# V in two products of eight heads, the gates' logits in a product of their own, and the first norm's transposes amid the output projection

## The chip, the cores and the metric

The kernel runs on one core of a Trainium2 chip. The metric is device time: microseconds (us) of one execution of the whole program. The time before is the median of three runs, 662.65 us (662.37 to 663.92). The engines are PE (TensorE, the matrix engine; PEld is its loading of weights), ACT (ScalarE), DVE (VectorE), POOL (GpSimd) and SP (SyncE, which here only issues DMAs).

## The reference

One layer of a trunk: forgetting attention, a normalisation, a gated MLP with a causal depthwise convolution, a second normalisation and a gated embedding. There are 512 tokens, a width of 1024, 16 heads of 64, an MLP of 2816, all in float32. Cut to what matters here:

```
proj = x @ w_in                                    # 1024 -> 3*1024 + 16
q, k, v, f_logit = jnp.split(proj, [D_MODEL, 2 * D_MODEL, 3 * D_MODEL], axis=-1)
log_f = jax.nn.log_sigmoid(f_logit + b_f)          # one gate a token and head
c = jnp.cumsum(log_f, axis=1)
s = q k^T / 8 + c[query] - c[key]                  # causal
o = softmax(s) v
x = layer_norm(ALPHA * x + o @ w_out)
x = layer_norm(ALPHA * x + conv_ffn(x))            # gelu(conv(x w_up_g)) * (x w_up_u), then w_down
return x + sigmoid(x @ w_gate + b_gate) * (p @ w_proj)
```

## The kernel before

**Split products.** Every float32 operand of PE is cut in two parts of a narrower type, a high one (a copy on ACT) and a low one (the rest, a subtraction on DVE). `three` (L110) then makes a product out of three matmuls: high by high, high by low, low by high. Its flag `weights_move` says which operand stands in PE and which streams through it: with the flag, 128 tokens of x (or of the heads' outputs) stand and up to 512 columns of weights stream.

**Weights.** The class `Weights` (L52) keeps a list of slabs in the order in which they are used. `load_to` issues their DMAs into four buffers `raw`; `cut_to` cuts the next slab into `whi` (ACT, L93) and `wlo` (DVE, L94), five buffers each; `get` cuts one slab ahead and loads three further ones ahead. All DMAs are issued by SP, one after the other in program order. The tile framework's scheduler sets each engine's order from the order of the code, and frees buffers and banks as their readers finish.

**Attention.** `value_rows(n)` (L280) computes V of a group of heads for all four tiles of 128 tokens, in four PSUM banks `pv`. There are three groups (`V_HEADS`, L40): 4, 6 and 6 heads. The first carries the 16 columns of the gates' logits along, so that its rows are 272 wide; the other two are 384 wide. The first group runs at the very start, while x itself is still arriving and being cut (`load_x`, `cut_x`); its slabs hold one, one, two, two and two of the eight blocks of 128 rows (`k`). Its logits stand with tokens on partitions; four transposes (L436) turn them into `pf`, heads on partitions, from which L437 to L450 make the cumulated gates `cr`. `project(m, s)` computes queries or keys of two heads (`pp`, 24 matmuls of 512 columns). Then a loop over heads does scores (`s`), softmax, transposes (`t`) and values (`o`), each step a head behind the one before. Half of the output projection (columns 0 to 511, banks `ao`, `out_first`) runs between the last heads.

**Output projection and first norm.** The loop at L535 does the other half, bank `ap`, one token tile t at a time: 24 matmuls, then on DVE the addition to `y` (L496), statistics (L503, L507, L508), with a power on POOL (L509), and the normalisation (L510, L511, each 128x1024). `flip(t)` (L513) turns a normalised tile around for the MLP: twice four transposes on PE into a bank `nt` (L518), a high copy on ACT (`x1h`, L522) and a low part on DVE (`x1l`, L523). In the loop `flip` of tiles 0 and 1 is called behind all that belongs to tiles 2 and 3 (L546). Then the PSUM pool of eight banks (`first`) is closed, and a second of six banks `b` and two banks `gu` is opened (L550, L551). `flip` of tile 2 follows (L637), and that of tile 3 stands between products of the MLP.

**MLP.** It goes in four parts of up to six column blocks f. `up(f, s)` computes the gate side `g` (s = 0) or the other side `u` (s = 1) of a block, 24 matmuls; block 0, and `g` of block 1, go in two halves of 256 tokens, the first two halves ahead of `flip` of tile 3. The banks of f < 6 have the tag `b`, the later ones `gu`. `conv(f)` makes `a` out of `g`; `product(f)` multiplies it with `u` into `E` (L577). From part 1 on, the down products of the part before are woven in.

Of the kernel before, what the change touches and what calls it, by code (L numbers as in the profile page):

```python
# [8 lines left out]
F32 = mybir.dt.float32  # L9
F32R = mybir.dt.float32r  # L10
BF16 = mybir.dt.bfloat16
AF = mybir.ActivationFunctionType
# [3 lines left out]
P = 128  # L16
S = 512
D = 1024
H = 16
DH = 64  # L20
F = 2816
PLE = 256
NT = S // P
KD = D // P
# [12 lines left out]
UNIT = 1024  # L37
WARM = 14

V_HEADS = ((0, 4), (4, 6), (10, 6))  # L40

OUT_FIRST = {14: (0, 1), 15: (2, 3), 16: (4,), 17: (5, 6)}
RAW_BUFS = 4
# [59 lines left out]


@with_exitstack
def trunk_layer(ctx: ExitStack, tc: tile.TileContext, xT, x2d, pT, wqk, wv0, wv1, wv2, bf, wo, wup, cwb,
                wdn, wpl, wg, bg, gm, bm, gf, bff, out):
    nc = tc.nc

# [9 lines left out]
    first = ExitStack()  # L119
    psum = [first.enter_context(tc.tile_pool(name="psum", bufs=8, space=bass.MemoryType.PSUM))]  # L120

    def bank(name, tag="b", bufs=None):
        return psum[-1].tile([P, 512], F32, tag=tag, name=name, bufs=bufs)
# [2 lines left out]
        return w[k0 * P:(k0 + n) * P, cols * 512:(cols + 1) * 512].rearrange("(k p) c -> p k c", p=P)  # L126

    W = Weights(nc, base)
    wv = (wv0, wv1, wv2)
    u_v, u_qk = {}, []  # L130

    def add_v(n, pieces):
        k0, w = 0, wv[n].shape[1]
        for c in pieces:
            src = wv[n][k0 * P:(k0 + c) * P, :].rearrange("(k p) c -> p k c", p=P)
            u = W.add(src, n=c * w, inner=w)
            for j in range(c):
                u_v[n, k0 + j] = u, slice(j * w, j * w + w)
            k0 += c

    add_v(0, (1, 1, 2, 2, 2))
    for m in range(KD):
        u_qk.append([W.add(wqk[m, s], inner=P) for s in range(2)])
        if m == 0:
            add_v(1, (2, 2, 2, 2))
            add_v(2, (2, 2, 2, 2))

    u_o = [[W.add(half_rows(wo, 2 * j, 2, n), inner=512) for j in range(4)] for n in range(2)]

# [119 lines left out]
    load_x(2)  # L269
    load_x(3)  # L270
    W.load_to(3)
    nc.sync.dma_start(bf_sb, bf)
    cut_x(0, slice(0, P))
    W.cut_to(1)
    cut_x(0, slice(P, S))

    logits = {}
    fl_all = ap.tile([P, 128], F32, name="f", bufs=1)

    def value_rows(n):  # L280
        h0, nh = V_HEADS[n]
        w = wv[n].shape[1]
        pv = [bank(f"pv{t}_{n}") for t in range(NT)]
        for k in range(KD):
            if n == 0:
                if k + 4 < KD:
                    load_x(k + 4)
                if k + 1 < KD:
                    cut_x(k + 1)
            u, c = u_v[n, k]  # L290
            hi, lo = W.get(u)
            for t in range(NT):
                tk = slice(t * P, (t + 1) * P)
                three(pv[t][:, :w], hi[:, c], lo[:, c], xh[:, k, tk], xl[:, k, tk], k == 0,
                      k == KD - 1, weights_move=True)
        for t in range(NT):
            if n == 0:
                logits[t] = fl_all[:, t * H:t * H + H]
                nc.scalar.activation(logits[t], pv[t][:, nh * DH:w], AF.Copy)
            v = V[:, t, h0:h0 + nh]  # L300
            p3 = pv[t][:, :nh * DH].rearrange("p (h d) -> p h d", d=DH)
            nc.scalar.activation(v[:, :, 0, :], p3, AF.Copy)
            nc.vector.tensor_sub(v[:, :, 1, :], p3, v[:, :, 0, :].bitcast(F32))

    value_rows(0)

    KB = [ap.tile([P, S], F32R, name=f"KB{i}", bufs=1) for i in range(2)]
    QB = [ap.tile([P, S], F32R, name=f"QB{i}", bufs=1) for i in range(2)]
# [122 lines left out]
    cr = ap.tile([H, 4, S], F32R, name="cr", bufs=1)  # L431
    fa = ap.tile([H, S], F32, tag="KA", name="fa")
    fb = ap.tile([H, S], F32, tag="QA", name="fb")
    pf = bank("pf")
    for t in range(NT):
        nc.tensor.transpose(pf[:H, t * P:(t + 1) * P], logits[t], ident)  # L436
    nc.scalar.activation(fa, pf[:H], AF.Identity, bias=bf_sb)  # L437
    nc.vector.tensor_scalar_min(fb, fa, 0.0)
    nc.vector.scalar_tensor_tensor(fa, fb, -2.0, fa, op0=ALU.mult, op1=ALU.add)
    nc.scalar.activation(fa, fa, AF.Exp, scale=-1.0)  # L440
# [12 lines left out]
    stack(0)  # L453
    value_rows(1)
    stack(1)
    value_rows(2)
    for h in range(H + 2):
        m, s = divmod(h, 2)
        if h == 2:
# [33 lines left out]
    def add_half(t, n, ps, first):  # L493
        c = slice(n * 512, (n + 1) * 512)
        if first:
            nc.vector.scalar_tensor_tensor(y[:, t, c], y[:, t, c], ALPHA, ps, op0=ALU.mult, op1=ALU.add)  # L496
        else:
            nc.vector.tensor_add(y[:, t, c], y[:, t, c], ps)
# [3 lines left out]
            stats[t] = post.tile([P, 2, 6], F32, tag="st", name=f"st{t}", bufs=NT)  # L502
        nc.vector.bn_stats(stats[t][:, n, :], y[:, t, n * 512:(n + 1) * 512])  # L503

    def norm(t, g, b):
        mv = post.tile([P, 4], F32, tag="mv", name="mv", bufs=2)
        nc.vector.bn_aggr(mv[:, 0:2], stats.pop(t))  # L507
        nc.vector.tensor_scalar_add(mv[:, 2:3], mv[:, 1:2], EPS)  # L508
        nc.gpsimd.tensor_tensor(mv[:, 3:4], mv[:, 2:3], neghalf, op=ALU.pow)  # L509
        nc.vector.scalar_tensor_tensor(y[:, t], y[:, t], mv[:, 0:1], g, op0=ALU.subtract, op1=ALU.mult)  # L510
        nc.vector.scalar_tensor_tensor(y[:, t], y[:, t], mv[:, 3:4], b, op0=ALU.mult, op1=ALU.add)  # L511

# [22 lines left out]
    for t in range(NT):  # L535
        ps = bank(f"ap{t}")
        tk = slice(t * P, (t + 1) * P)
        for k in range(KD):
            hi, lo = W.get(u_o[1][k // 2])
            c = slice(k % 2 * 512, k % 2 * 512 + 512)  # L540
            three(ps, hi[:, c], lo[:, c], oh[:, k, tk], ol[:, k, tk], k == 0, k == KD - 1,
                  weights_move=True)
        add_half(t, 1, ps, True)
        half_stats(t, 1)
        norm(t, g1, b1)
        if t > 1:  # L546
            flip(t - 2, x1h, x1l)
    rows.close()
    oT.close()
    first.close()  # L550
    psum.append(ctx.enter_context(tc.tile_pool(name="psum2", bufs=6, space=bass.MemoryType.PSUM)))  # L551


    hpool = ctx.enter_context(tc.tile_pool(name="hpool", bufs=1, side="right"))
# [79 lines left out]
                        give(b, half, c)  # L634
                yield

    flip(2, x1h, x1l)  # L637
    before = None
    for part in range(4):
        if part < 3:  # L640
            shape = [P, len(PAIRS[0]), 7 * HALF]
        else:
            shape = [P, len(REST), S]
        hh, hl = [hpool.tile(shape, F32R, tag=g, name=f"{g}{part}", bufs=2) for g in ("hh", "hl")]
        slots = iter(CHUNKS[part] or ())

        def between():
            for _ in range(next(slots, 0)):
                next(before)

        for f in range(6 * part, min(6 * part + 6, NF)):
            q, j = f % 2, f // 2
            if q == 0:
                E = hpool.tile([P, 8 * HALF], F32, tag="E", name=f"E{j}")
            if f == 0:
                a, b = slice(0, HALF), slice(HALF, S)
                up(0, 0, a)
                up(0, 1, a)
                flip(3, x1h, x1l)
                up(1, 0, a)  # L660
                up(0, 0, b)
                up(0, 1, b)
                up(1, 0, b)
                conv(0)
                product(0, E[:, :S])
                continue
            if f > 1:
                up(f, 0)
            conv(f)
            between()  # L670
            up(f, 1)
            product(f, E[:, q * S:(q + 1) * S])
            if q:
                if part < 3:
                    operands(hh, hl, j - 3 * part, E)
                else:
                    i = f - 1 - REST[0]
                    e = E[:, :2 * S].rearrange("p (a b) -> p a b", b=S)
                    nc.scalar.activation(hh[:, i:i + 2], e, AF.Copy)
                    nc.vector.tensor_sub(hl[:, i:i + 2], e, hh[:, i:i + 2].bitcast(F32))  # L680
            between()
        if part < 3:
            before = down(part, hh, hl)
# [79 lines left out]
def _layout(a):  # L763
    import numpy as np

    c = np.ascontiguousarray
    w_in = a["attn_w_in"][0]
    qk = w_in[:, :2 * D].reshape(KD, P, 2, KD, P).transpose(3, 2, 1, 0, 4)
    wv = [w_in[:, 2 * D + h * DH:2 * D + (h + n) * DH] for h, n in V_HEADS]
    up = a["ffn_w_up"][0].reshape(KD, P, 2, NF, P).transpose(3, 2, 1, 0, 4)  # L770
    cw = np.concatenate([a["ffn_conv_w"][0], a["ffn_conv_b"][0][None]], 0)
    return {
        "xT": c(a["x"][0].T),
        "x2d": c(a["x"][0]),
        "pT": c(a["p"][0, 0].T),
        "wqk": c(qk),
        "wv0": c(np.concatenate([wv[0], w_in[:, 3 * D:]], 1)),
        "wv1": c(wv[1]),
        "wv2": c(wv[2]),
        "bf": c(a["attn_b_f"][0][:, None]),  # L780
        "wo": c(a["attn_w_out"][0]),
        "wup": c(up),
        "cwb": c(cw.reshape(4, NF, P).transpose(2, 1, 0)),
        "wdn": c(a["ffn_w_down"][0]),
        "wpl": c(a["ple_w_proj"][0]),
        "wg": c(a["ple_w_gate"][0]),
        "bg": c(a["ple_b_gate"][0][None]),
        "gm": c(a["ln_mix_g"][0][None]),
        "bm": c(a["ln_mix_b"][0][None]),
        "gf": c(a["ln_ffn_g"][0][None]),  # L790
        "bff": c(a["ln_ffn_b"][0][None]),
    }
# [16 lines left out]
```

## Time and profile before

The profiled execution took 664.75 us, 2.1 more than the median of the timed ones. Its trace spans 663.0 us.

| what | value |
|---|---|
| median of the timed runs | 662.65 us |
| profiled execution | 664.75 us |
| its span | 663.0 us |
| mean granted clock of PE | 0.997 |
| POOL's largest group, L377, softmax scaling | 72.9 us |
| DVE's largest group, L94, low parts of weights | 143.2 us |
| moved by DMA | 76.95 MB, mean 116 GB/s |

The busy time of an engine says how much of the span it worked; PE's matmuls overlap a little, so the length of a group of them is read from the chain of waits or from a timeline, not from the mean of one. In a timeline a row has its start, its length, the engine, the line, the operation and the operands, and in brackets how long the engine stood still ahead of it and for whom. The granted clock is the share of full speed at which PE ran.

### The profile page before, as it was taken

The page shows a single profiled execution, that of the slowest core. Times are in us where ns is not written, and L with a number is a line of the kernel's source. Part 1 is how long each engine was busy: PE and PEld are TensorE (multiplying, and loading weights), DVE is VectorE, ACT ScalarE, POOL GpSimd, SP SyncE. Part 2 cuts the span into 40 slices and gives each one's busy share as a digit, 9 for nine tenths or more (in the row PEclk, how much of TensorE's full clock was granted, in tenths as well). Part 3 has the DMA queues.
Part 4 walks back from the last instruction along what each step waited for, and adds up shares of the span by engine and source line. Part 5 has one row for each costly group of instructions (what it writes and reads, how often), then busy time and mean ns, then how long its engine had stood idle before and what let it go on. Part 6 is the DMA issues. An engine that isn't in the chain of part 4 may idle for free.

```text
span 663.0 us, 8693 instructions
## 1 busy us (share of the span) xinstructions
PE 654.0 (99%) x3234; PEld 558.0 (84%) x3234; DVE 474.0 (71%) x746; ACT 309.9 (47%) x511; POOL 85.2 (13%) x78
## 2 busy tenths in 40 slices
PE   8999999999999989999999999999999999999997
PEld 7899888888888879888888888888888888888886
DVE  7674789999986694755776675877667857599364
ACT  5653677787774232534434334443425343426231
POOL 0000554445444020000000000000000000012000
PEclk9999999999999998999999999999999999999999
DMA  8533221112262312322244244443363444562321
GB/s 272 176 129 128 64 66 64 40 61 66 66 228 74 128 54 77 128 96 95 86 137 160 95 153 134 158 128 111 96 189 111 129 142 128 158 223 65 102 81 47
DMA packets 32890, 76.95 MB, mean 116 GB/s; under 512 B 2960, under 2 KB 6800, under 8 KB 32848
## 3 DMA queue, kind: packets, MB, share of 16 engines
q1 hardware_dynamic: 32848, 76.41, 35.4%
q8 instruction: 25, 0.41, 0.3%
q14 instruction: 17, 0.14, 0.1%
HBM read 74.17 MB, written 2.10 MB: 115 GB/s over the span
## 4 chain that ended last, share of the span: by engine, by line
PE 95%; DVE 1%; ACT 1%; DMA 1%; issue 1%; SPq 0%; DVEq 0%
PE g L115 18%; PE u L115 18%; PE pp L115 13%; PE x L115 7%; PE gt L115 7%; PE pv L115 6%; PE z L115 4%; PE ao L115 3%; PE r L115 3%; PE o L403 3%; PE t L390 2%; PE ap L115 2%; PE y L115 2%; PE pl L115 2%; PE s L359 2%; PE s L361 1%
## 5 line engine op out<-in xcount | busy, mean ns | idle before, releaser
L93 ACT ACTIVATE whi<-raw 128x1024 fp32r<-128x1024 f32 (+5 forms) x131 | 126.3, 964 | 183.9 <-PE g L115 64.5
L94 DVE TENSOR_TENSOR wlo<-raw,whi 128x1024 fp32r<-128x1024 f32 (+5 forms) x131 | 143.2, 1099 | 67.7 <-ACT whi L93 67.1
L377 POOL TENSOR_SCALAR pr<-pr,rl 128x128 f32<-128x128 f32 (+1 forms) x64 | 72.9, 1157 | 134.7 <-DVE rl L373 134.7
L115 PE MATMUL g<-x1h,whi 128*128 128x512 f32 (+1 forms) x192 | 71.9, 375 | 0.0
L115 PE MATMUL g<-x1l,whi 128*128 128x512 f32 (+1 forms) x192 | 71.6, 373 | 0.0
L115 PE MATMUL g<-x1h,wlo 128*128 128x512 f32 (+1 forms) x192 | 71.6, 373 | 0.0
L115 PE MATMUL u<-x1h,whi 128*128 128x512 f32 (+1 forms) x184 | 69.9, 380 | 0.0
L115 PE MATMUL u<-x1l,whi 128*128 128x512 f32 (+1 forms) x184 | 69.9, 380 | 0.0
L115 PE MATMUL u<-x1h,wlo 128*128 128x512 f32 (+1 forms) x184 | 69.9, 380 | 0.0
L509 POOL TENSOR_TENSOR mv<-mv,neghalf 128x1 f32<-128x1 f32 x8 | 11.6, 1447 | 387.0 <-DVE mv L508 364.7
L115 PE MATMUL pp<-xh,wlo 128*128 128x512 f32 x128 | 50.2, 392 | 0.0
L115 PE MATMUL pp<-xl,whi 128*128 128x512 f32 x128 | 50.0, 391 | 0.0
L115 PE MATMUL pp<-xh,whi 128*128 128x512 f32 x128 | 49.9, 390 | 0.0
L115 PEld LDWEIGHTS g<-x1l,whi 128*128 128x128 f32 x192 | 36.6, 190 | 6.3
L115 PEld LDWEIGHTS g<-x1h,whi 128*128 128x128 f32 x192 | 36.6, 190 | 6.2
L115 PEld LDWEIGHTS g<-x1h,wlo 128*128 128x128 f32 x192 | 36.5, 190 | 6.2
L369 ACT ACTIVATE pr<-s,nm 128x128 f32<-128x128 f32 (+1 forms) x64 | 33.5, 526 | 16.9 <-DVE nm L368 15.8
L115 PEld LDWEIGHTS u<-x1l,whi 128*128 128x128 f32 x184 | 34.6, 188 | 6.6
L115 PEld LDWEIGHTS u<-x1h,whi 128*128 128x128 f32 x184 | 34.6, 188 | 6.5
L115 PEld LDWEIGHTS u<-x1h,wlo 128*128 128x128 f32 x184 | 34.6, 188 | 6.5
L577 DVE TENSOR_TENSOR E<-a,u 128x512 f32<-128x512 f32 x22 | 15.1, 687 | 34.2 <-PE u L115 33.4
L115 PE MATMUL pv<-whi,xh 128*128 128x384 f32 (+1 forms) x96 | 30.4, 330 | 1.1 <-ACT whi L93 1.1
(173 smaller groups left out, 1419.9 us busy)
## 6 DMA issues: line engine op xcount, KB each, us to landing
raw<-wup SPq DMA_DIRECT2D x44, 512.0 KB
raw<-wdn SPq DMA_DIRECT2D x31, 512.0 KB
raw<-wqk SPq DMA_DIRECT2D x16, 512.0 KB
raw<-wo SPq DMA_DIRECT2D x8, 512.0 KB
raw<-wg SPq DMA_DIRECT2D x8, 512.0 KB
raw<-wv SPq DMA_DIRECT2D x8, 384.0 KB
side<-wdn SPq DMA_DIRECT2D x9, 256.0 KB
raw<-wdn SPq DMA_DIRECT2D x9, 256.0 KB
```

The source lines that it names most:

```text
L93: self.nc.scalar.activation(hi[:, c:e], piece, AF.Copy)
L94: self.nc.vector.tensor_sub(lo[:, c:e], piece, hi[:, c:e].bitcast(F32))
L115: nc.tensor.matmul(ps, lhsT, rhs, start=start and n == 0, stop=stop and n == 2, skip_group_check=on)
L359: nc.tensor.matmul(ps[:, :n], QA[:, q], KA[:, :n], start=True, stop=False)
L361: nc.tensor.matmul(ps[:, :n], qb[0:68, q], kb[0:68, :n], start=False, stop=True)
L369: nc.scalar.activation(pr[:, off:off + w], ps[:, :w], AF.Exp, bias=nm[:, i:i + 1], accum_out=ls[:, i:i + 1])
L377: nc.gpsimd.tensor_scalar_mul(pr[:, off:off + w], pr[:, off:off + w], rl[:, i:i + 1])
L390: nc.tensor.transpose(ps[:, w:w + P], pr[:, o:o + P], ident)
L403: nc.tensor.matmul(ps[:, q0:], V[:, j, h], p[:, o:o + w], start=j == 0 and n == 0, stop=j == NT - 1 and n == 1)
L509: nc.gpsimd.tensor_tensor(mv[:, 3:4], mv[:, 2:3], neghalf, op=ALU.pow)
L577: nc.vector.tensor_mul(e, gates.pop(f), ups.pop((f, 1)))
```

## The change

V comes in two groups of eight heads, whose rows are 512 columns wide, a whole PSUM bank. The first has slabs of one, one, two, two and two blocks as before, the second four slabs of two. The logits get a product of their own behind the first group of V: a small tensor `fw` of 64 columns holds the high parts of their 16 weight columns in columns 0 to 15, the low parts in columns 32 to 47, and zeros elsewhere. `fw` stands in PE while x streams through it, 512 tokens at a time, low and high, for eight blocks: 16 matmuls. The result has heads on partitions, high part in rows 0 to 15 and low part in rows 32 to 47, which are added on DVE; the transposes and the copies of the logits are gone. In the output projection `flip` of tiles 0 and 1 moves ahead into the product of tiles 2 and 3, behind k = 3, and `flip` of tile 2 into `norm` of tile 3, ahead of its two normalising operations. The exchange of the PSUM pools moves from there to the start of part 1 of the MLP.

```
-V_HEADS = ((0, 4), (4, 6), (10, 6))
+V_HEADS = ((0, 8), (8, 8))
...
 @with_exitstack
-def trunk_layer(ctx: ExitStack, tc: tile.TileContext, xT, x2d, pT, wqk, wv0, wv1, wv2, bf, wo, wup, cwb,
+def trunk_layer(ctx: ExitStack, tc: tile.TileContext, xT, x2d, pT, wqk, wv0, wv1, wf, bf, wo, wup, cwb,
                 wdn, wpl, wg, bg, gm, bm, gf, bff, out):
...
     W = Weights(nc, base)
-    wv = (wv0, wv1, wv2)
+    wv = (wv0, wv1)
     u_v, u_qk = {}, []
...
             add_v(1, (2, 2, 2, 2))
-            add_v(2, (2, 2, 2, 2))
...
     W.load_to(3)
-    nc.sync.dma_start(bf_sb, bf)
     cut_x(0, slice(0, P))
...
-    logits = {}
-    fl_all = ap.tile([P, 128], F32, name="f", bufs=1)
+    wf_raw = ap.tile([P, KD * H], F32, name="wf", bufs=1)
...
         for t in range(NT):
-            if n == 0:
-                logits[t] = fl_all[:, t * H:t * H + H]
-                nc.scalar.activation(logits[t], pv[t][:, nh * DH:w], AF.Copy)
             v = V[:, t, h0:h0 + nh]
...
     value_rows(0)
+
+
+    nc.sync.dma_start(wf_raw, wf)
+    nc.sync.dma_start(bf_sb, bf)
+    fw = ap.tile([P, KD, 64], F32R, tag="QA", name="fw")
+    nc.vector.memset(fw.bitcast(F32), 0.0)
+    wf3 = wf_raw.rearrange("p (k h) -> p k h", h=H)
+    nc.scalar.activation(fw[:, :, 0:H], wf3, AF.Copy)
+    nc.vector.tensor_sub(fw[:, :, 32:32 + H], wf3, fw[:, :, 0:H].bitcast(F32))
+    pf = bank("pf")
+    for k in range(KD):
+        for n, x in enumerate((xl, xh)):
+            nc.tensor.matmul(pf[:64], fw[:, k, :], x[:, k, :], start=k == 0 and n == 0,
+                             stop=k == KD - 1 and n == 1)
...
     fb = ap.tile([H, S], F32, tag="QA", name="fb")
-    pf = bank("pf")
-    for t in range(NT):
-        nc.tensor.transpose(pf[:H, t * P:(t + 1) * P], logits[t], ident)
     nc.scalar.activation(fa, pf[:H], AF.Identity, bias=bf_sb)
+    nc.vector.tensor_add(fa, pf[32:32 + H], fa)
     nc.vector.tensor_scalar_min(fb, fa, 0.0)
...
     stack(1)
-    value_rows(2)
     for h in range(H + 2):
...
-    def norm(t, g, b):
+    def norm(t, g, b, meanwhile=None):
         mv = post.tile([P, 4], F32, tag="mv", name="mv", bufs=2)
...
         nc.gpsimd.tensor_tensor(mv[:, 3:4], mv[:, 2:3], neghalf, op=ALU.pow)
+        if meanwhile is not None:
+            flip(*meanwhile)
         nc.vector.scalar_tensor_tensor(y[:, t], y[:, t], mv[:, 0:1], g, op0=ALU.subtract, op1=ALU.mult)
...
                   weights_move=True)
+            if t > 1 and k == 3:
+                flip(t - 2, x1h, x1l)
         add_half(t, 1, ps, True)
         half_stats(t, 1)
-        norm(t, g1, b1)
-        if t > 1:
-            flip(t - 2, x1h, x1l)
+        norm(t, g1, b1, (2, x1h, x1l) if t == 3 else None)
     rows.close()
     oT.close()
-    first.close()
-    psum.append(ctx.enter_context(tc.tile_pool(name="psum2", bufs=6, space=bass.MemoryType.PSUM)))
...
-    flip(2, x1h, x1l)
     before = None
     for part in range(4):
+        if part == 1:
+            first.close()
+            psum.append(ctx.enter_context(tc.tile_pool(name="psum2", bufs=6, space=bass.MemoryType.PSUM)))
         if part < 3:
...
         "wqk": c(qk),
-        "wv0": c(np.concatenate([wv[0], w_in[:, 3 * D:]], 1)),
+        "wv0": c(wv[0]),
         "wv1": c(wv[1]),
-        "wv2": c(wv[2]),
+        "wf": c(w_in[:, 3 * D:].reshape(KD, P, H).transpose(1, 0, 2).reshape(P, KD * H)),
         "bf": c(a["attn_b_f"][0][:, None]),
```

On PE, at the end of the first group of V, this stood before (`pp_0` and `pp_1` are queries and keys of the first two heads; the three rows of a product repeat for each k):

```order
L115 MATMUL pp_0_317<-xh,wlo_254 128x512
L115 MATMUL pp_0_317<-xl,whi_253 128x512
L115 MATMUL pp_0_317<-xh,whi_253 128x512
L436 MATMUL pf<-ident,f 16x128 x4
L115 MATMUL pp_1_370<-xh,wlo_312 128x512
```

And now, there and at the end of `pv`:

```order
L115 MATMUL pv_0_131<-whi_218,xh 128x512
L115 MATMUL pv_0_131<-whi_218,xl 128x512
L115 MATMUL pv_0_131<-wlo_219,xh 128x512
L312 MATMUL pf<-xl,fw 64x512
L312 MATMUL pf<-xh,fw 64x512
...
L115 MATMUL pp_0_335<-xh,wlo_253 128x512
```

The four small transposes between queries and keys are gone; 16 matmuls of 512 columns stand ahead of both. The first group of V has 96 matmuls as before, now of 512 columns instead of 272; behind the keys there are 96 of 512 columns instead of 192 of 384.

On PE, from the output projection's last two tiles to the MLP's first product, this stood before (`ap_2532` is tile 2, `ap_2579` tile 3):

```order
L115 MATMUL ap_2532<-wlo_2468,oh 128x512
L518 MATMUL nt<-ident,y 128x128 x8
L115 MATMUL ap_2579<-whi_2371,oh 128x512
...
L115 MATMUL ap_2579<-wlo_2468,oh 128x512
L518 MATMUL nt<-ident,y 128x128 x16
L115 MATMUL g_2652<-x1h,whi_2479 128x256
```

And now (`ap_2414` is tile 2, `ap_2461` tile 3):

```order
L115 MATMUL ap_2414<-wlo_2326,oh 128x512
L525 MATMUL nt<-ident,y 128x128 x8
L115 MATMUL ap_2414<-whi_2337,oh 128x512
...
L115 MATMUL ap_2461<-wlo_2326,oh 128x512
L525 MATMUL nt<-ident,y 128x128 x8
L115 MATMUL ap_2461<-whi_2337,oh 128x512
...
L115 MATMUL ap_2461<-wlo_2350,oh 128x512
L525 MATMUL nt<-ident,y 128x128 x8
L115 MATMUL g_2530<-x1h,whi_2361 128x256
```

Two of the three groups of transposes now stand inside the products of tiles 2 and 3, 12 matmuls before their ends, and one group, not two, stands between the last product and the MLP.

On DVE the same stretch ends so before, from the last addition to the statistics of tile 3:

```order
L511 SCALAR_TENSOR_TENSOR y<-y,mv,b_2416 128x1024
L94 TENSOR_TENSOR wlo_2658<-raw_2471,whi_2657 128x1024
L496 SCALAR_TENSOR_TENSOR y<-y,ap_2579 128x512
L523 TENSOR_TENSOR x1l<-nt,x1h 128x4x128
L503 BN_STATS st_2440<-y 128x6
```

And now:

```order
L518 SCALAR_TENSOR_TENSOR y<-y,mv,b_2298 128x1024
L530 TENSOR_TENSOR x1l<-nt,x1h 128x4x128 x2
L501 SCALAR_TENSOR_TENSOR y<-y,ap_2461 128x512
L94 TENSOR_TENSOR wlo_2536<-raw_2353,whi_2535 128x1024
L508 BN_STATS st_2322<-y 128x6
L530 TENSOR_TENSOR x1l<-nt,x1h 128x4x128
```

Both low parts of tile 1 stand ahead of tile 3's addition, where before they stood behind it; the cut of a slab of weights stands between that addition and its statistics, and the low parts of tile 2 follow.

On PE, at the start of part 1 of the MLP, with what a row waits for in brackets (`u_3134` and `u_3012` are `u` of f = 5, `g_3175` and `g_3057` are `g` of f = 6), this stood before:

```order
L115 MATMUL u_3134<-x1l,whi_3067 128x512
L115 MATMUL u_3134<-x1h,wlo_3068 128x512
L115 MATMUL g_3175<-x1h,whi_3099 128x512 [waits Activation_49]
L115 MATMUL g_3175<-x1l,whi_3099 128x512
L115 MATMUL g_3175<-x1h,wlo_3100 128x512 [waits DVE_49]
```

And now:

```order
L115 MATMUL u_3012<-x1l,whi_2945 128x512
L115 MATMUL u_3012<-x1h,wlo_2946 128x512
L115 MATMUL g_3057<-x1h,whi_2977 128x512 [waits DVE_49]
L115 MATMUL g_3057<-x1l,whi_2977 128x512
L115 MATMUL g_3057<-x1h,wlo_2978 128x512
```

The products stand in the same order. Before, the first waited for the high part of its slab (ACT) and the third for the low part (DVE); now the first waits for DVE, at a count that is reached with the product `E` of f = 5 (L577 before, L582 now).

## The prediction

> **What bounds the kernel now.** I read each engine's share first, then the waits of PE, then the chain of waits in order of time, then the timelines of the three places that the change touches.
>
> ```profile
> PE 654.0 (99%) x3234; PEld 558.0 (84%) x3234; DVE 474.0 (71%) x746; ACT 309.9 (47%) x511; POOL 85.2 (13%) x78
> PE nt L518 <- DVE x1l L523: 2.7, 1, 2.7
> PE pv L115 <- ACT whi L93: 1.1, 2, 0.9
> PE warm L223 <- DVE zeros L219: 1.1, 1, 1.1
> ```
>
> PE is busy for 654.0 of 663.0 us (first line). The waits of PE (us in all, times, longest) name two besides the one ahead of the warm-up: 1.1 us for the first weights, 2.7 us at one group of transposes. So a change is worth what it takes out of PE's own stream and out of PE's waits; the other engines count where PE comes to wait for them.
>
> **What a product costs PE.** Durations of single matmuls overlap, so I take groups from the chain of waits: start, length, what, count.
>
> ```profile
> 17.81 1.51 PE pv L115 x12
> 25.16 0.44 PE pf L436 x4
> 25.60 5.46 PE pp L115 x24
> 31.06 33.30 PE pv L115 x192
> 225.02 14.07 PE ap L115 x62
> ```
>
> A 272-column product costs 1.51/12 = 0.126 us, one of 384 columns 33.30/192 = 0.173, one of 512 columns 0.227 (5.46/24, and 14.07/62 with x standing and the weights moving, the form of the new pv). Before: 96 x 0.126 + 192 x 0.173 = 45.4 us, and 0.4 for the four transposes of the logits. After: 192 x 0.227 = 43.6 us for V and 16 x 0.227 = 3.6 for the logits. No row shows 64 columns of weights standing; the bounds are 0.126 and 0.30 each, 2.0 to 4.8 us in all, and I take the 512-column price, since the moving side has that length. Sum: 47.2 - 45.8 = **1.4 us more PE work**: the logits' own product costs more than the 96 fewer products of V save.
>
> The Trainium skill, page "TensorE: Matmul & The Clock Gate", section "Wait — 56ns, not 53.3ns?", gives N/2.4 GHz plus about 2.5 ns from one warm matmul to the next. By that 272, 384 and 512 columns are 116, 163 and 216 ns, and the same sum comes to 2.2 us more. The rows above lie 11 to 13 ns over N/2.4 GHz, so here dropping a product is worth more than by the page, and the measured price stays.
>
> **The start.** Here PE waits for data, and the slabs of weights grow.
>
> ```profile
> 3.94 0.59 PE L115 MATMUL pv<-whi,xh 128*128 128x272 f32 x1
> 6.15 0.43 PE L115 MATMUL pv<-wlo,xh 128*128 128x272 f32 x1
> 6.38 0.42 PE L115 MATMUL pv<-whi,xl 128*128 128x272 f32 x1
> 10.29 0.39 PE L115 MATMUL pv<-whi,xh 128*128 128x272 f32 x1 [0.94 <-ACT whi L93]
> 4.07 5.49 DMA raw<-wv
> 9.58 0.66 ACT L93 ACTIVATE whi<-raw 128x544 fp32r<-128x544 f32 x1
> 13.65 1.06 ACT L93 ACTIVATE whi<-raw 128x1024 fp32r<-128x1024 f32 x1 [0.72 <-PE pv L115]
> 7.36:10.29 2.93, 1.99 (x12) 1.59 (x12) 1.82 (x4) 1.97 (x4) 0.00 (x0) 1.00 1.05 348
> 64.20 0.40 PE L359 MATMUL s<-KA,QA 128*128 128x256 f32 x2
> ```
>
> The third slab (k = 2 and 3) lands at 9.56 and is cut until 10.24; PE starts on it at 10.29 after 0.94 us of waiting and then runs without a gap to the first scores at 64.20. After the change the first three slabs carry 4 x 128 x 240 x 4 bytes = 0.49 MB more. At the 348 GB/s of that stretch (last column) this is 1.4 us, and the cut takes 1.06 for 0.66. So PE starts on it at 10.29 + 1.4 + 0.4 = 12.1, and I add 0.1 for its low half. Behind it stand 72 + 16 + 48 + 96 = 232 products of 512 columns, 52.6 us: first scores at 64.8, **+0.6 us**. Some of the 1.4 is paid out of the old wait.
> Lower bound: the slab is never late. The first product starts at about 4.5 (0.6 for the larger first slab and its cut); until 6.6 products run at half pace (6.15 to 6.38 is 0.23 us for 272 columns, against 0.126 later), that is five of them, and the other 19 of the first two slabs take 4.3: third slab at 11.0, so -0.6. Upper bound: the start loses as much as before (64.20 - 45.8 - 48 x 0.227 = 7.5 us), so the whole 1.4, and 0.6 more for a late slab: +2.0. The price of the logits (-1.6 to +1.2) adds to both ends.
> At nothing I cost the loads of the logits' weights and of the bias, which now stand on SP between two slabs of the second product, the clearing and splitting of fw, the extra addition on the gates' chain, and the wider evictions of V: they lie beside 52.6 us of products, and their results are asked for at about 28.5 (pf) and 64.8 (scores). Without that cover each is one operation of under 1.3 us.
>
> **The transposes of the first norm.** First PE, then one stretch's granted clock (the third column from the end), then DVE.
>
> ```profile
> 238.92 1.03 PE L518 MATMUL nt<-ident,y 128*128 128x128 f32 x8
> 239.71 0.48 PE L115 MATMUL ap<-whi,oh 128*128 128x512 f32 x1
> 248.96 1.96 PE L518 MATMUL nt<-ident,y 128*128 128x128 f32 x8 [2.67 <-DVE x1l L523]
> 250.57 0.56 PE L115 MATMUL g<-x1h,whi 128*128 128x256 f32 x1
> 254.33 0.28 PE L115 MATMUL u<-x1h,whi 128*128 128x256 f32 x1
> 257.21 1.03 PE L518 MATMUL nt<-ident,y 128*128 128x128 f32 x8
> 249.00:250.00 1.00, 1.00 (x5) 1.00 (x6) 1.00 (x2) 0.00 (x0) 0.00 (x0) 0.50 0.19 74
> 239.12 0.69 DVE L496 SCALAR_TENSOR_TENSOR y<-y,ap 128x512 f32<-128x512 f32 x1 [0.30 <-PE ap L115]
> 241.77 1.27 DVE L510 SCALAR_TENSOR_TENSOR y<-y,mv,g 128x1024 f32<-128x1024 f32 x1
> 242.96 1.22 DVE L94 TENSOR_TENSOR wlo<-raw,whi 128x1024 fp32r<-128x1024 f32 x1
> 244.10 1.28 DVE L511 SCALAR_TENSOR_TENSOR y<-y,mv,b 128x1024 f32<-128x1024 f32 x1
> 246.43 0.68 DVE L496 SCALAR_TENSOR_TENSOR y<-y,ap 128x512 f32<-128x512 f32 x1
> 247.03 0.68 DVE L523 TENSOR_TENSOR x1l<-nt,x1h 128x512 fp32r<-128x512 f32 x1
> 247.63 0.68 DVE L503 BATCH_NORM_STATS2 st<-y 128x6 f32<-128x512 f32 x1
> 251.88 1.27 DVE L511 SCALAR_TENSOR_TENSOR y<-y,mv,b 128x1024 f32<-128x1024 f32 x1
> ```
>
> The third group (tile t=2) waits 2.67 us for the last split of the second: the new PSUM pool takes nothing until the old one is read out. Behind it the clock is at 0.50: the eight transposes take 1.61 us (to 250.57) where they took 0.79 (238.92 to 239.71), and the 24 products of g 3.76 where the u group, 254.33 to 257.21, takes 2.88. So 2.67 + 0.82 + 0.88 = 4.4 us are lost.
> After: the same pool stays open, and two groups stand inside ap. The third product block ends 0.79 later than 245.2, at 246.0; the third group needs tile 2's norm. On DVE its first addition moves by one group to 239.9; L510 comes 2.65 - 2 x 0.60 behind (two splits leave the middle), I allow 1.8; L511 ends 2.33 + 1.28 later, 245.3. So group three runs at 246.0 without waiting, and g and u of half the tokens follow from 246.8 until 252.6 (2 x 2.88).
> The fourth group needs tile 3's norm. Its addition waits for the two splits of the second group (2 x 0.60 from 245.2): 246.4. Before, from there to the end of L511 it was 251.88 + 1.27 - 246.43 = 6.7 us; now one more cut (1.14) stands in it and one split (0.60) fewer, 7.3: 253.7. So PE waits 1.1 us at the fourth group, which starts at 253.75 where it stood at 257.21: **-3.5 us**. DVE is what is late next. Bounds: no wait there, 252.6, -4.6; a DVE chain 1 us longer, -2.5. The splits of the third and the fourth group lie beside products of the first 256 tokens, those of the fourth beside 2.88 us of g of f=1.
>
> **The pool is closed later.** The exchange of PSUM pools moves to the start of part 1, in front of g of f=6. The built order has its first matmul wait for DVE's product of f=5 (L577), which reads the last bank of the old pool; before, that matmul waited for no such thing.
>
> ```profile
> 318.74 5.44 PE g L115 x24
> 319.20 0.69 DVE L166 TENSOR_TENSOR raw<-raw,side 128x512 f32<-128x512 f32 x1 [2.33 <-DMA raw<-wdn]
> 319.81 0.68 DVE L577 TENSOR_TENSOR E<-a,u 128x512 f32<-128x512 f32 x1
> ```
>
> PE goes from u of f=5 to g of f=6 at 318.74 without a gap; the product runs from 319.81 to 320.49, held up by a load of wdn and the subtraction L166 ahead of it. With the 0.06 from the end of a split to PE (248.90 to 248.96), g starts at 320.55: **+1.8 us**. Queued behind it on PE is all of part 1, and all of it comes 1.8 us later. Bounds: +1.0 if L166 is early (0.68 and the hand-over), +3.5 if the clock drops behind it too (1.7, from above).
>
> **Sum.** 0.6 - 3.5 + 1.8 = **-1.1 us**. The profiled execution took 664.75 us, 663.0 of it span; it becomes 663.65. It lies 2.1 over the median of the timed runs, 662.65, so I put the difference there: **661.6 us**. A difference of 0.3% (2.0 us) is about what can be told from none.
>
> **Rivals.**
> - *DVE keeps up, and the slabs are in time*: -0.6 - 4.6 + 1.8 = -3.4, **659.3**. For it: PE waits for data only 1.1 us in all at the start. Against: DVE is nearly without a gap from 239 to 254. Chance 0.17.
> - *The supply of the first slabs decides*: +2.0 at the start, so +0.3, **662.9**. For it: 348 GB/s at a DMA share of 1.05, nothing to spare. Against: 512-column rows ask for fewer slabs per us once running. 0.10.
> - *The wait only moves*: the fourth group waits another 1.8 us for DVE, and the gain there is 1.7: +0.7, **663.3**. 0.05.
> - *The clock halves behind both new waits* (1.1 and 1.8 us): 1.7 each, so +2.3, **664.9**, slower. It decides from a length of wait between 0.94 us, behind which products ran at 0.126, and 2.67, behind which the clock was 0.50. For it: the second new wait lies midway between the two. Against: the first lies at the harmless end, and ahead of both stand products without a gap, where ahead of the 2.67 stood transposes. 0.08.
>
> The last rival turns on that page's section "Part 1: The HAM clock gate (the "warmup" mystery)" of the Trainium skill, by which the clock halves after an idle window of about 3.4 us, and on "Part 4: PE-mode transpose", by which transposes do not count as busy. The trace agrees: from the last product of ap (245.02) to 248.96 there are only transposes and waiting, nearly 3.6 us. By that rule both new waits are too short, and the time would be the forecast's.
>
> **How the numbers follow.** The forecast has 0.60, with 660.1 to 663.2 as its own range. Faster by over 0.3% is the first rival and a tenth of the forecast, 0.23; slower by over 0.3% is the last, 0.08; the rest, 0.69, lies between. The range runs from the first rival to beyond the third, 659.3 to 664.0; the last rival and the far ends of the bounds are left out.
>
> **What would show it.** pv in groups at 0.227 and pf near 3.6 us; first scores near 64.8; PE's waits naming nt <- L518 near 1 us, not x1l, and g of f=6 <- DVE E near 1.8; granted clock 1.00 in both places. Wrong if pf products cost under 0.15 us, if the third slab comes after 13, if g of f=6 doesn't wait, or if a row of 0.50 stands behind either wait.

## The result and the profile after

The changed kernel takes 664.18 us in the median of 22 runs (663.18 to 666.25), the kernel before beside it 663.68 us (22 runs, 662.37 to 664.33). The ratio is 1.0016, with an interval of 1.0009 to 1.0024: a little slower, by less than 0.3%, where 1.1 us of gain were forecast. The profiled execution took 665.8 us, 663.9 of it span; the one before 664.75 and 663.0. One execution of the kernel before, timed beside v_only below, took 938.18 us at a mean granted clock of 0.655; it is in none of the ratios and counts here.

First the engines' shares and the waits of PE in the changed kernel (us in all, times, longest):

```profile
PE 654.9 (99%) x3150; PEld 548.7 (83%) x3150; DVE 475.2 (72%) x741; ACT 308.1 (46%) x500; POOL 85.0 (13%) x78
PE g L115 <- DVE E L582: 1.8, 1, 1.8
PE pv L115 <- ACT whi L93: 1.0, 2, 0.8
PE nt L525 <- DVE y L518: 0.9, 1, 0.9
```

The wait of 2.7 us for x1l is gone. In its place stand two new ones, where and about as long as the prediction had them: 0.9 us for the norm of tile 3 and 1.8 us for the product E of f=5. Now the chain of waits (start, length, what, count):

```profile
4.07 6.34 DMA raw<-wv
11.53 1.24 DVE wlo L94
12.81 15.75 PE pv L115 x68
28.56 3.68 PE pf L312 x16
43.14 21.76 PE pv L115 x96
317.77 7.34 PE g L115 x24
```

The logits' product costs 3.68/16 = 0.230 us a matmul, V in 512 columns 21.76/96 = 0.227. The first three lines are the third slab of V's weights: it lands at 10.41 us, and PE runs on without a gap from 12.81, behind its low part on DVE. The last line is the one that was not in the sum: 24 products of g take 7.34 us there, where each such group elsewhere takes 5.44. The timeline of that place, DVE and PE, and the stretch behind it (granted clock third from the end):

```profile
316.42 0.69 DVE L165 TENSOR_TENSOR raw<-raw,side 128x512 f32<-128x512 f32 x1 [2.36 <-DMA raw<-wdn]
317.03 0.68 DVE L582 TENSOR_TENSOR E<-a,u 128x512 f32<-128x512 f32 x1
317.77 0.50 PE L115 MATMUL g<-x1h,whi 128*128 128x512 f32 x1 [1.84 <-DVE E L582]
319.00:321.00 2.00, 2.00 (x7) 1.54 (x6) 1.54 (x4) 0.39 (x1) 0.00 (x0) 0.50 0.57 190
```

E stands behind L165 on DVE, which waits for a load; PE waits 1.84 us for E; and behind that wait the clock is at 0.50. The products there take 7.34 - 5.44 = 1.90 us more, so the place costs 3.74 us, not 1.8.

### The profile page after: what moved, and what is told of

It is laid out like the page before. It is cut to its first block, busy times and chain, and to the rows that moved or that the text cites. A ratio compares the mean times of both kernels' runs of the same rounds, so it can differ in the third digit from the quotient of the medians.

```text
span 663.9 us, 8484 instructions
## 1 busy us (share of the span) xinstructions
PE 654.9 (99%) x3150; PEld 548.7 (83%) x3150; DVE 475.2 (72%) x741; ACT 308.1 (46%) x500; POOL 85.0 (13%) x78
## 4 chain that ended last, share of the span: by engine, by line
PE 88%; issue 4%; DVE 3%; DMA 2%; ACT 1%; POOL 1%; SPq 0%; POOLq 0%; DVEq 0%
PE g L115 18%; PE u L115 17%; PE pp L115 13%; PE x L115 7%; PE gt L115 7%; PE pv L115 6%; PE z L115 4%; PE r L115 3%; PE o L411 2%; PE t L398 2%; PE y L115 2%; PE ao L115 2%; PE pl L115 2%; PE s L367 2%; PE s L369 1%
## 5 line engine op out<-in xcount | busy, mean ns | idle before, releaser
L93 ACT ACTIVATE whi<-raw 128x1024 fp32r<-128x1024 f32 (+1 forms) x127 | 125.3, 987 | 188.6 <-PE g L115 66.5
L94 DVE TENSOR_TENSOR wlo<-raw,whi 128x1024 fp32r<-128x1024 f32 (+1 forms) x127 | 142.7, 1127 | 69.9 <-ACT whi L93 69.3
L582 DVE TENSOR_TENSOR E<-a,u 128x512 f32<-128x512 f32 x22 | 15.1, 686 | 34.3 <-PE u L115 33.6
L115 PEld LDWEIGHTS pp<-xh,whi 128*128 128x128 f32 x128 | 24.0, 188 | 5.1
```

Source lines behind the costliest of these rows:

```text
L93: self.nc.scalar.activation(hi[:, c:e], piece, AF.Copy)
L94: self.nc.vector.tensor_sub(lo[:, c:e], piece, hi[:, c:e].bitcast(F32))
L115: nc.tensor.matmul(ps, lhsT, rhs, start=start and n == 0, stop=stop and n == 2, skip_group_check=on)
L582: nc.vector.tensor_mul(e, gates.pop(f), ups.pop((f, 1)))
```

## The experiments

The table puts all traces side by side. The second column is the start of the first scores (s). The next two are counted from there, so that the scatter of the start drops out: the fourth group of transposes (tile 3), and the first down product x, which stands behind g of f=6. "0.50" names the wait behind which the trace shows the clock halved. "Low" counts the timed runs whose mean granted clock over the execution is 0.997 or less; all others have 0.998 to 1.000. The counted runs of the kernel before are those timed beside the experiments, since its first 22 have no clock on record.

| kernel | s | 4th group | x | 0.50 behind | low | median us | ratio to before |
|---|---|---|---|---|---|---|---|
| before | 64.20 | 193.01 | 259.82 | x1l, 2.67 us | 56 of 79 | 663.68 | |
| before_again | 63.49 | 192.97 | 259.78 | x1l, 2.67 us | 1 of 1 | 664.01 (one) | |
| after | 64.74 | 189.60 | 260.20 | E, 1.84 us | 8 of 22 | 664.18 | 1.0016 (1.0009 to 1.0024) |
| again | 64.45 | 189.52 | 258.41 | none | 3 of 10 | 664.19 | 1.0018 (1.0005 to 1.0032) |
| side_pool | 64.01 | 189.58 | 257.60 | none | 0 of 10 | 663.09 | 0.9995 (0.9983 to 1.0007) |
| fill | 64.53 | 189.56 | 258.86 | none | 0 of 10 | 664.15 | 1.0012 (1.0000 to 1.0023) |
| one_pool | 65.21 | 193.59 | 260.46 | none | 3 of 6 | 666.84 | 1.0051 (1.0033 to 1.0069) |
| same_pool | 64.36 | 189.56 | 256.43 | none | 0 of 10 | 661.55 | 0.9975 (0.9964 to 0.9987) |
| v_only | 64.90 | 191.39 | 258.20 | none | 6 of 12 | 664.38 | 1.0010 (0.9999 to 1.0021) |
| flips_close | 63.09 | 193.38 | 260.19 | g, 3.05 us | 9 of 10 | 664.29 | 1.0010 (0.9999 to 1.0022) |
| close_only | 63.38 | 189.12 | 258.14 | none | 4 of 10 | 662.63 | 0.9989 (0.9978 to 1.0000) |
| flips_same | 63.50 | 189.62 | 256.50 | none | 0 of 6 | 660.92 | 0.9965 (0.9952 to 0.9979) |
| stay | 63.75 | 189.16 | 255.97 | none | 0 of 5 | 660.12 | 0.9945 (0.9932 to 0.9959) |
| v_stay | 64.20 | 189.14 | 255.95 | none | 0 of 5 | 660.83 | 0.9960 (0.9947 to 0.9972) |

**Is the halved clock a part of every execution?** Both kernels once more, with no edit.

> The changed kernel once more, nothing altered. Theory A (the exchange of the PSUM pools costs a wait of 1.84 us for DVE's product E of f=5 and, behind it, a stretch at clock 0.50 that costs 1.90 us more): the wait shows again at 1.8 us, the stretch too, span near 663.9 us. Rival B (the stretch at 0.50 falls where some window happens to stand, independent of this wait): the wait shows again, but in this execution no 0.50 stands behind it, and the span is near 662.0 us.

> The kernel before once more, nothing altered. Theory F (the stretch at 0.50 behind the wait for x1l comes in some executions and not in others, as behind the wait for E): wait of 2.7 us again; if there is no row of 0.50 behind it, the span is 1.7 us shorter, near 661.3 us. Rival (it is part of every execution of this kernel): 0.50 again, span near 663.0 us.

The changed kernel again: PE at g of f=6, the same place in the chain of waits, and the stretch behind it:

```profile
317.26 0.50 PE L115 MATMUL g<-x1h,whi 128*128 128x512 f32 x1 [1.70 <-DVE E L582]
317.26 5.76 PE g L115 x24
319.00:321.00 2.00, 2.00 (x10) 1.67 (x9) 1.04 (x3) 0.89 (x1) 0.00 (x0) 1.00 0.78 240
```

The same program has the wait, and no halving, as rival B expected; the span is 661.8 us, 2.1 less than in the first trace. That the stretch is independent of the wait, rival B's reason, this trace doesn't show, and the counts below speak against it. At a clock of 1.00 the 24 products take 5.76 us here, still 0.32 more than elsewhere. So of the 1.90 us in the first trace 0.3 come with the stop itself and 7.34 - 5.76 = 1.6 with the halved clock. The kernel before showed its stretch a second time, so that run decides nothing by itself; v_only, below, has the same wait of 2.67 us at the same place:

```profile
249.61 1.09 PE L523 MATMUL nt<-ident,y 128*128 128x128 f32 x8 [2.67 <-DVE x1l L528]
250.00:251.00 1.00, 1.00 (x11) 1.00 (x10) 1.00 (x3) 0.70 (x2) 0.03 (x1) 1.00 0.01 4
```

There the clock stays at 1.00. So the stretch is no fixed part of either kernel. The page "TensorE: Matmul & The Clock Gate" of the Trainium skill, section "Part 1: The HAM clock gate (the "warmup" mystery)", says that activity is judged in a window that runs free of the program; by that, the same wait falls well or badly from one execution to the next, and the traces agree. The same section asks for an idle window of some 3.4 us; here 1.84 us between two rows of products did it once, so the measurement decides.

The timed runs have no trace, but each run listed in the column "low" has its mean granted clock. A stretch shows in it: the four traces that have one have a mean of 0.997, the ten others 0.999 or 1.000. By it the 79 runs of the kernel before fall in two groups whose times don't overlap: 56 low ones, from 663.24 us up, and 23 others, up to 663.05. Its first 22 runs, which have only times, fall the same way: 8 lie from 662.37 to 662.96, 14 from 663.52 to 664.33, and none between. The 22 of the changed kernel do so too: 14 from 663.18 to 664.66 (median 663.92), and 8 low ones from 664.96 to 666.25 (median 665.88).

So the kernels can be compared at equal clock, and then the change costs more than the medians say. Among the first 22 it is 1.3 us without a stretch (663.92 against 662.66) and 2.0 with one (665.88 against 663.84); among the runs of again and those beside it, 1.7 (664.08 against 662.35) and 2.0 (665.99 against 663.96). The median of the changed kernel lies among the runs without a stretch, that of the kernel before among those with one.

**Is the wait what sets the clock off?** In fill PE works through the wait; in side_pool the subtraction ahead of E goes to POOL. The first three added lines are the edit of fill, the pair below that of side_pool.

```
+            spare = bank("spare")
+            for _ in range(16):
+                nc.tensor.matmul(spare[:, :256], idle[:, :P], idle, start=True, stop=True)
             first.close()
...
-                nc.vector.tensor_sub(t1, t1, t2)
+                (nc.gpsimd if part == 0 and i == 0 else nc.vector).tensor_sub(t1, t1, t2)
```

> The changed kernel with 16 idle matmuls (zeros, 256 columns) into a spare bank between u of f=5 and the exchange, so that PE works through its wait of 1.84 us. Theory A (the idle time makes the clock halve): no row of 0.50 near 318 us, 1.9 us less than the changed kernel, span near 662.0 us, ratio near 0.9985. Rival B (the clock halves for another reason, as the load or the place in time): the stretch at 0.50 stays and the span is near 663.9 us.

> The changed kernel with the one subtraction L165 that stands ahead of E of f=5 on DVE given to POOL. E runs about 1.0 us earlier, so g of f=6 waits about 0.8 us. Theory A with a bound of length between 0.94 and 1.84 us: clock stays at 1.00, 2.9 us less than the changed kernel, span near 661.0 us, ratio near 0.997. Rival D (any wait there halves the clock): a stretch at 0.50 remains, 1.0 us less, span near 662.9 us.

First the filled wait, then the other kernel:

```profile
315.52 1.92 PE L647 MATMUL spare<-zeros 128*128 128x256 bf16 x16
317.87 0.47 PE L115 MATMUL g<-x1h,whi 128*128 128x512 f32 x1 [0.43 <-DVE E L582]
```

```profile
316.03 0.50 PE L115 MATMUL g<-x1h,whi 128*128 128x512 f32 x1 [0.85 <-DVE E L582]
```

The traces alone settle nothing: neither shows a stretch, but again has none either. The mean clocks do. Of the 32 runs of the changed kernel (after and again) 11 are low, of the 20 with the wait filled or shortened none; if the 11 fell at random among all 52, they would spare those 20 in about 2 of 1000 cases. So theory A is borne out for the clock: it halves behind the wait, and not behind one of 0.85 us (none of ten runs). Which run it strikes stays open. Fill saves no time against a run without a stretch, since its x comes 0.45 us later than in again (258.86 against 258.41). In side_pool the wait fell from 1.70 to 0.85 us, as expected; the median is 1.1 us lower than that of again.

All the kernels together say how the odds go with the wait, taking its length in a kernel's timed runs to be that of its traces. Behind 2.67 or 3.05 us (before, v_only, flips_close) 71 of 101 runs are low, behind 1.70 to 1.92 us (after, again, close_only) 15 of 42, and in the six kernels whose longest wait behind the warm-up is at most 0.9 us (side_pool, fill, same_pool, flips_same, stay, v_stay) none of 46. Length is not the only difference: ahead of the longest waits stand transposes, ahead of the others products. And one_pool warns against a rule on single waits: its longest in the trace is 0.89 us, but three (0.32, 0.57 and 0.89) come within 2.5 us, and 3 of its 6 runs are low; whether those three waits do it isn't shown.

In side_pool part of the gain was lost again: x started 0.81 us earlier than in again, yet a later product x, at 548 us, waits 0.75 us for DVE.

**Without the exchange.** One_pool had six banks of one tag and two of another from the start, dealt out in turn (the first piece below); same_pool simply keeps the eight banks (the rest).

```
+                turns[0] += 1
+                if turns[0] % 4 == 0:
+                    tag, bufs = "gu", 2
...
-        if part == 1:
-            first.close()
-            psum.append(ctx.enter_context(tc.tile_pool(name="psum2", bufs=6, space=bass.MemoryType.PSUM)))
...
-            ups[f, s] = bank(f"{'gu'[s]}{f}", *(() if f < 6 else ("gu", 2)))
+            ups[f, s] = bank(f"{'gu'[s]}{f}")
```

> The changed kernel without any exchange of PSUM pools: one pool from the start, six banks b and two banks gu, every fourth bank of the attention and of part 0 taken from gu. Theory A: g of f=6 waits for nothing, the clock stays at 1.00, 3.7 us less than the changed kernel: span near 660.2 us, ratio to the kernel before near 0.9955. Rival C (the wait moves to the next bank that is not free, at the first products of down or at the attention): a new wait of over 1 us on PE, span 662 us or more.

> The changed kernel without an exchange: the pool of eight banks stays to the end, and the blocks f = 6 and up take their banks from it too. Up to g of f=6 PE's order is that of the changed kernel. Theory A: g of f=6 no longer waits, the clock stays at 1.00, so 1.7 to 1.8 us less than the changed kernel where that showed no stretch at 0.50 (span 661.8 us) and 3.7 less where it did: span near 660.1 us, ratio near 0.9965. Rival C (the wait moves to the next bank in turn): PE waits over 0.5 us at x, y, z, g or u behind 315 us, and the span is 661 us or more.

One_pool ended as rival C: no wait for E, but PE waits three times, 1.8 us in all, in the attention for softmax's last step, which no other trace shows, and the fourth group comes 193.59 us behind the first scores, 4.1 later than in again. What else the new turn of banks changed there stays open. Same_pool bears out theory A: no wait for E, x at 256.43 instead of 258.41, and no new wait. By the medians it takes 2.6 us less than the changed kernel.

**The part at V.** V_only is the kernel before with this part of the change alone; v_stay is the same with the pool of eight banks kept to the end, and stay has that pool with the old V.

```
-V_HEADS = ((0, 4), (4, 6), (10, 6))
+V_HEADS = ((0, 8), (8, 8))
...
+            nc.tensor.matmul(pf[:64], fw[:, k, :], x[:, k, :], start=k == 0 and n == 0,
+                             stop=k == KD - 1 and n == 1)
```

> Only the part of the change at V: two products of eight heads, logits in a product of their own; the transposes and the exchange of the pools as in the kernel before. Theory A: it costs what stood between the traces at the first scores and at the output projection, 0.4 to 0.7 us, so a ratio near 1.0008; first scores near 64.6 us. Rival E (V costs nothing, the difference at the start is the run's own scatter): ratio 1.000 within 0.0005, first scores at 64.2 us or earlier.

> The same with V in two products of eight heads and the logits in a product of their own. Neither has a wait behind which the clock has halved, so the difference between the two is the price of that part alone. Theory A: 0.9 us more than without it (the mean of the first scores in seven traces with it, 64.6 us, and in five without, 63.5 us, differ by 0.9 to 1.1 us): span near 659.5 us, ratio 0.0014 higher. Rival E (it costs nothing): the same span within 0.3 us.

With the clock's scatter, v_only is not clear of no change (0.9999 to 1.0021). At equal clock it is 1.2 us slower than the kernel before beside it without a stretch (663.62 against 662.41), 0.8 with one (664.78 against 663.99). Between stay and v_stay, which have no such wait, the cost is clear: 660.12 and 660.83 us, ranges that don't touch, 0.7 us of cost. In the spans it is 0.4; the first scores start at 63.09 to 64.20 in the six traces of the old V (mean 63.57) and at 64.01 to 65.21 in the eight of the new (64.55).

**The transposes and the place of the exchange, apart.** All with the old V: flips_close moves only the transposes, close_only only the exchange, flips_same moves the transposes and drops the exchange, stay drops the exchange and nothing else. Below, the first piece is from flips_close, the other two are from close_only; stay drops the closing and the tag gu as same_pool does.

```
+            if t > 1 and k == 3:
+                flip(t - 2, x1h, x1l)
...
     oT.close()
-    first.close()
...
     for part in range(4):
+        if part == 1:
+            first.close()
```

> The kernel before with only the transposes moved amid the output projection; the exchange of the pools stays ahead of the MLP. Theory A: g of f=0 then waits for the low part of the third group (it ends 250.7 us in the trace of the changed kernel, where g starts at 247.5): a wait of about 3 us, often with a stretch at 0.50, and no wait at f=6; span 661.3 us without a stretch, 663 with one, ratio between 0.999 and 1.002. Rival H (the transposes alone bring the gain): ratio 0.997 or less.

> The kernel before with only the exchange of the PSUM pools moved to the start of part 1; V, logits and transposes as before. Theory A: the third group of transposes no longer waits for x1l, but the first g behind it does, so that the fourth group comes about 1.3 us earlier than in an execution of the kernel before without a stretch at 0.50; the wait for E of f=5, 1.8 us, takes more than that back: span near 661.8 us where no 0.50 shows, ratio near 1.0005. Rival G (the old place of the exchange was the whole cost, and the wait for E is hidden with the old order of DVE): ratio 0.997 or less.

The transposes alone, PE at the first g and the clock behind it:

```profile
249.12 0.39 PE L115 MATMUL g<-x1h,whi 128*128 128x256 f32 x1 [3.05 <-DVE mv L508]
250.00:251.00 1.00, 1.00 (x7) 1.00 (x7) 1.00 (x2) 0.00 (x0) 0.73 (x1) 0.50 0.03 8
```

The built order has this g wait for the low part of the third group (to 249.07); the view names the short operation behind it on DVE. The wait has only moved from the transposes to g, and the fourth group comes as late as before (193.38 against 193.01). Theory A. The exchange alone, PE:

```profile
246.89 0.39 PE L115 MATMUL g<-x1l,whi 128*128 128x256 f32 x1 [0.37 <-DVE x1l L523]
252.50 1.04 PE L518 MATMUL nt<-ident,y 128*128 128x128 f32 x8
315.94 0.50 PE L115 MATMUL g<-x1h,whi 128*128 128x512 f32 x1 [1.92 <-DVE E L575]
```

Both theories missed. With the transposes where they were, g waits 0.37 us, not 2.67 - 1.3 = 1.4, since only the product that needs the low part waits, not the pool. The fourth group comes 189.12 us behind the first scores, 0.4 to 0.5 earlier than where the transposes had been moved, and waits for nothing. The wait for E is there, 1.92 us. So the place of the transposes brought nothing; that led to a third theory, I.

> The kernel before with the transposes amid the output projection, and without any exchange (the pool of eight banks to the end); V and the logits as before. Theory A: the gain of the transposes without the two costs: 1.5 us less than the kernel before where that shows no stretch at 0.50, 3.2 us less where it does; span near 659.7 us, ratio near 0.9960. Rival C: waits elsewhere eat it, span 661 us or more.

> The kernel before with no exchange of the PSUM pools and nothing else changed: eight banks to the end, V, logits and the transposes' place as before. Theory I (the place of the transposes is worth nothing, all of the gain lies in the exchange that no longer stands ahead of them): what the kernel with the exchange moved shows (span 660.5 us) less its wait of 1.9 us for E, so a span near 658.6 us and a ratio near 0.995, below the kernel with the transposes moved and no exchange (659.1 us). Rival H (the transposes amid the projection bring a part of the gain): span 659.6 us or more.

First flips_same, PE and DVE, then stay:

```profile
253.12 1.09 PE L520 MATMUL nt<-ident,y 128*128 128x128 f32 x8 [0.88 <-DVE y L513]
245.81 0.68 DVE L496 SCALAR_TENSOR_TENSOR y<-y,ap 128x512 f32<-128x512 f32 x1
246.40 1.22 DVE L94 TENSOR_TENSOR wlo<-raw,whi 128x1024 fp32r<-128x1024 f32 x1
250.65 1.22 DVE L94 TENSOR_TENSOR wlo<-raw,whi 128x1024 fp32r<-128x1024 f32 x1
251.79 1.28 DVE L513 SCALAR_TENSOR_TENSOR y<-y,mv,b 128x1024 f32<-128x1024 f32 x1
```

```profile
252.91 1.04 PE L518 MATMUL nt<-ident,y 128*128 128x128 f32 x8
244.82 1.22 DVE L94 TENSOR_TENSOR wlo<-raw,whi 128x1024 fp32r<-128x1024 f32 x1
245.96 0.68 DVE L496 SCALAR_TENSOR_TENSOR y<-y,ap 128x512 f32<-128x512 f32 x1
250.87 1.27 DVE L511 SCALAR_TENSOR_TENSOR y<-y,mv,b 128x1024 f32<-128x1024 f32 x1
252.07 2.35 DVE L94 TENSOR_TENSOR wlo<-raw,whi 128x1024 fp32r<-128x1024 f32 x2
314.28 0.39 PE L115 MATMUL g<-x1h,whi 128*128 128x512 f32 x1
```

With the transposes amid the projection, DVE does two cuts of weights (L94) between tile 3's addition (L496) and its last normalising step, and PE waits 0.88 us for that step. With the transposes behind, no cut stands between the two: one is done ahead of the addition, at 244.82, the next ones behind the step. It ends at 252.14, and PE, which is there at 252.91, doesn't wait. At f=6 g starts without waiting. Theory I holds: span 658.7 us where 658.6 was expected, ratio 0.9945. Stay beats both kernels, by the one edit of not exchanging the pool: by 3.75 us in the medians, and by 2.5 against the two runs of the kernel before beside it that have no stretch (660.12 against 662.62).

## Why the prediction was wrong

- **The start, +0.6: near, in part by luck.** A matmul of pf takes 0.230 us and one of pv 0.227, where 0.227 was taken, and the first scores start at 64.74 where 64.8 was forecast. The way there was another: the third slab landed at 10.41 us, half a microsecond ahead of 9.56 + 1.4 = 10.96, and its low part, priced at 0.1 behind the cut (12.2), was done at 12.77. And the 64.20 that the sum started from is the latest first score of the six traces of the old V. The part at V costs 0.7 us in the clean pair and 0.8 to 1.2 in v_only; the means of the first scores differ by 1.0. The remark that the rows lie 11 to 13 ns over N/2.4 GHz is off by about one: the same rows give 12.5 to 14. No term hangs on it.
- **The transposes, -3.5: right in this pair of traces, not for every run.** The fourth group came 3.4 us earlier against the first scores (193.01 to 189.60), and PE waited 0.88 us there for DVE where 1.1 was forecast. A step that failed is the one that reads "2.67 + 0.82 + 0.88 = 4.4 us are lost": the wait was there in all three traces that have the old order (before, before_again, v_only), but 0.82 and 0.88 are the halved clock but for 0.1 (193.01 - 191.39 = 1.62 us against v_only), which 56 of 79 runs of the kernel before had. Between v_only and again, both without a stretch, the gain is 191.39 - 189.52 = 1.87 us.
- **The pool closed later, +1.8: right as a wait, too small as a price.** The other step that failed, and the larger. The wait measured 1.84 and 1.70 us. But the 0.3 us that the products behind the stop take longer stood in no term, and the 1.6 us of halved clock only in the last rival, at a chance of 0.08 and together with the other wait. The halving came behind this wait alone, in one of two traces and, by the mean clock, in 11 of 32 runs. So the place costs 2.0 us without a stretch (1.70 + 0.32) and 3.7 with one. Over all runs that is about 2.0 + 1.6 x 11/32 = 2.6 us where 1.8 was taken; the transposes bring 1.9 + 1.6 x 56/79 = 3.0 where 3.5 was.
- **The sum.** Without stretches it is +1.0 - 1.9 + 2.0 = +1.1 us instead of -1.1; the runs without a stretch show +1.3 and +1.7. With one in both kernels it is +1.0 - 3.4 + 3.7 = +1.3; those runs show 2.0. What the rest is, 0.2 to 0.7 us, stays open. The medians differ by only 0.5 us, since they compare unlike runs; the ratio says 0.0016 x 663 = 1.1.
- **The base, too.** The gain was taken off 662.65 us, the median of three runs, two of which lie in the lower of the two clusters; with 22 runs it is 663.68. So a gain that held a stretch was subtracted from a time of the cluster without one.
- **What the prediction didn't separate:** it credited one step with what the transposes' place and the pool did together. The pool did all of it; the new place of the transposes takes 0.4 to 0.5 us away.

## What to carry to other kernels

A wait in one profile has two parts here: the time that the engine stood, which came back in every trace of the same program, and a slower clock behind it, which did not; price them apart. Before a sum rests on the second part, take a second trace, and sort the timed runs by their mean granted clock: it says which of them had it, and lets two kernels be compared at equal clock. A wait at a pool's exchange goes with the exchange: before moving it to another place, ask whether the old pool can simply stay. When a change has two edits that serve one aim, price each without the other.

## What the hardware showed beyond that

The halved clock lasted 3.4 us in each of the four traces that show it: from 249.0 to 252.4 us in the kernel before, 248.2 to 251.6 in before_again, 249.4 to 252.8 in flips_close and 318.7 to 322.1 in the changed kernel, by the granted clock of stretches of a tenth of a microsecond. It began within 0.1 us of PE's return in the first two, 0.3 us after it in flips_close, and almost 1 us after it in the changed kernel. Waits up to 0.94 us had no such stretch in these traces, the one ahead of the warm-up left aside; 1.70 and 1.92 us had none, 1.84 us had one, 2.67 us had one twice and none once, 3.05 us had one.
